# Sums of the weight quarters: from accumulating DMAs in DRAM to VectorE in the raw tiles

## The chip, the cores and the metric

One core of one Trainium2 chip runs the whole program in one launch. The metric is the device time in microseconds (us). Engines are called by these names: TensorE (PE: matmuls; PEld: its weight loads), VectorE (DVE), ScalarE (ACT), GpSimd (POOL) and SyncE (SP). SyncE and GpSimd issue the DMAs.

## The reference

A streaming-encoder block on 1024 tokens of width 1024, with 16 learned meta tokens ahead of them. The normalised stream is multiplied by `w_in`; its columns give, for four mLSTM heads (0 to 3) and four retention heads (4 to 7), queries, keys, values and an output gate. Each head runs a chunked scan over time and a norm, is gated, and `w_out` brings the heads back. A gated MLP with a causal convolution follows.

```python
    proj = up @ w_in
    (ml_q, ml_k, ml_v, ml_o, ml_i, ml_f, rt_q, rt_k, rt_v, rt_g) = jnp.split(proj, offs, axis=-1)
    ...
    h_ml = jax.nn.sigmoid(ml_o.astype(jnp.float32)) * h_ml
    ...
    h_rt = jax.nn.silu(rt_g.astype(jnp.float32)) * h_rt
    mixed = jnp.concatenate([h_ml, h_rt], axis=-1).astype(u.dtype)
    return (mixed @ w_out)[:, n_pad:]
```

Everything is float32.

## The kernel before, in words

**Products.** A float32 matrix is split into two float32r parts, `hi` (a cast on ScalarE) and `lo` (the rest, a subtraction on VectorE), and a product is three matmuls, hi x hi, hi x lo, lo x hi (`mm3s`). Most large products use the seven products of Strassen's scheme in Winograd's form: a weight is cut into four quarters, and seven products of quarters, or of sums of quarters, with blocks of the stream replace eight. The sums of the stream (S1 to S4) are made once; the sums of the weights, T1 = W11 + W12, T2 = T1 + W22, T3 = W12 + W22 and T4 = W21 + T2, are made for every head.

**Stages.** After a first norm (0 to about 82 us) the heads run from about 82 to 866 us in the order 4, then pairs (0, 1), (2, 3), (5, 6), then 7. For head 4 queries and keys come from plain products (`q4_group`). For the others `wino_fm("q", h)` makes queries and keys, `wino_fm("o", h)` the gate; `v_steps(p)` makes the values of a pair. Each of these is seven products in the order of `ROWS`. A head's products are merged with the scan tasks of the head before (`merge`, `group`), so that TensorE has both. From 866 us the output projection and the MLP follow; a planner with a model of the chip's times then orders each engine's queue from what the program emits, and each engine works through its own queue in that order.

**Weights on their way.** All loads stand in one list, `units`. `need(key, ahead)` issues units up to the one that is needed and two more. A unit takes a raw tile (`raw`, 128 x 1024 float32, 512 KB, two in a ring), loads it by SyncE's queue (L199), casts it into a tile `hi` (L201) and subtracts into a tile `lo` (L202). There are three pairs of tiles `hi`, `lo`, of 128 x 1024 each. A head of `wino_fm` has four units: W11 with W21, two units of sums, and W22 alone (half a tile). Between them stand, in the same ring, the `m` units (`last_two`: the last two tokens' part of `w_out`, scaled on ScalarE into a pair of split tiles and added to `accd` in DRAM by GpSimd, L243) and the `r` units (`first_right`: splits a block of the mixed heads and stores it).

**Weight sums.** `insum` makes the sums of one weight in DRAM by GpSimd's queue: a copy of the four quarters to `gs` (for values `vs`; L264), then four accumulating DMAs (`add`, L248). `job()` issues one weight's sums, at the start of the next group of heads. The same queue makes the sums of `w_out` and `w_down` (`wsum`; L255, L248).

**Meta tokens.** The values of the 16 meta tokens are made from the unsplit weights: `meta()` loads `w_vp[p]` again, in eight pieces of 256 KB through two halves of a slot (`vm`, L611), and multiplies by `ug` (L614).

**Scan.** `scan_b` copies the numerator out of the bank `num` on ScalarE (L1079) and the denominator's column `den` on VectorE (L1081).

Of the kernel before, what the change touches and what calls it, by code (L numbers as in the profile page):

```python
# [17 lines left out]
P = 128  # L18
# [7 lines left out]
DV = 256  # L26
# [39 lines left out]
def body(ctx, tc, h_in, vecs, cst, mask_in, rot, w_v0, w_vp, w_g, w_out, w_up, w_gate, w_down, out):  # L66
# [52 lines left out]
    vz = st.tile([P, 2, DV], F32, name="vz")  # L119
# [38 lines left out]
    nc.scalar.activation(warm[:, 0:1], epsc, AF.Square)  # L158
    for i in range(2):
        nc.sync.dma_start(w0raw[i], w_v0[i])  # L160
    nc.sync.dma_start(cs, cst)
# [16 lines left out]
    def unit(key, src, n=UN):  # L178
        units.append((key, src, n))
# [6 lines left out]

    def issue(upto):
        while issued[0] < min(upto, len(units)):
            u = units[issued[0]]
            issued[0] += 1  # L190
            if callable(u[1]):
                ready[u[0]] = u[1]()
                continue
            key, src, n = u
            nm = "_".join(str(k) for k in key)
            raw = raw_tile(nm)
            c = n // len(src)
            for i, x in enumerate(src):
                nc.sync.dma_start(raw[:, i * c:(i + 1) * c], x)  # L199
            hi, lo = split_tiles(nm)  # L200
            nc.scalar.copy(hi[:, :n], raw[:, :n])  # L201
            nc.vector.tensor_tensor(lo[:, :n], raw[:, :n], hi[:, :n].bitcast(F32), ALU.subtract)  # L202
            ready[key] = (hi, lo, raw)
# [12 lines left out]
    gsum = {i: dram.tile([P, 4 * HB], F32, name=f"gs{i}") for i in range(1, 17)}  # L216
# [3 lines left out]
    def u_fm(kind, h, extra=()):  # L220
        i = GI[kind, h]
        w, q = w_g[i], gsum[i]
        a = [[w[:, HB:3 * HB]], [q[:, :2 * HB]], [q[:, 2 * HB:]], [w[:, :HB]]]
        for j, x in enumerate(a):
            unit((kind, h, j), x, UN if j < 3 else HB)
            if j in (1, 2) and len(extra) > j - 1:
                units.append(extra[j - 1])

    def u_vp(p):
        w, q = w_vp[p], vsum[p]  # L230
        for j, (x, o) in enumerate(((w, 1), (w, 2), (q, 0), (q, 1), (q, 3), (w, 0), (q, 2))):
            unit(("vp", p, j), [x[:, o * UN:(o + 1) * UN]])

    def last_two(k):
        raw = raw_tile(f"m{k}")
        nc.sync.dma_start(raw, w_out[k])
        for t, x in enumerate(split_tiles(f"m{k}")):
            x = x.bitcast(F32)
            nc.scalar.activation(x, raw, AF.Copy, scale=mm[:, k, t:t + 1])
            if k == 8:  # L240
                nc.sync.dma_start(accd[t], x)
            else:
                G.dma_start(accd[t], x, accum_op=ALU.add)  # L243
# [17 lines left out]
    def insum(w, q, n, cuts):  # L261
        for i in range(cuts):
            c = 4 * n // cuts
            dep(G.dma_start(q[:, i * c:(i + 1) * c], w[:, i * c:(i + 1) * c]), last["pace"], True)  # L264
        b = lambda x, o: x[:, o * n:(o + 1) * n]
# [5 lines left out]
    jobs = []  # L271

    def job():
        if jobs:
            jobs.pop(0)()

    def j_fm(kind, h):
        i = GI[kind, h]
        jobs.append(lambda: insum(w_g[i], gsum[i], HB, 1))

    def j_vp(p):
        jobs.append(lambda: insum(w_vp[p], vsum[p], UN, 2))
# [6 lines left out]
    def first_right(k):  # L289
        a = raw_tile(f"fr{k}")  # L290
        hi, lo = split_tiles(f"fr{k}")
        nc.sync.dma_start(a, mxd[k])
        nc.scalar.copy(hi[:, :HB], a[:, :HB])
        nc.vector.tensor_tensor(lo[:, :HB], a[:, :HB], hi[:, :HB].bitcast(F32), ALU.subtract)
        nc.vector.tensor_tensor(a[:, HB:], a[:, :HB], a[:, HB:], ALU.subtract)
        nc.sync.dma_start(rone[k][:, :HB], hi[:, :HB].bitcast(F32))
        nc.sync.dma_start(rone[k][:, HB:], lo[:, :HB].bitcast(F32))
        nc.sync.dma_start(diff[k], a[:, HB:])
# [3 lines left out]
    def m_units(h):  # L302
        return [(("m", h, b), lambda k=2 * h + b: last_two(k), 0) for b in range(2)]

    def r_units(*ks):
        return [(("r", k), lambda k=k: first_right(k), 0) for k in ks]

    q4 = w_g[GI["q", 4]]
    unit(("q4", 0), [q4[:, HB:3 * HB]])
    unit(("q4", 1), [q4[:, 3 * HB:], q4[:, :HB]])  # L310
# [9 lines left out]
    u_fm("q", 7, r_units(2, 3))  # L320
    u_fm("v", 7, r_units(4, 5))
    u_fm("o", 7, m_units(6))
    units += r_units(6, 7)
# [59 lines left out]
    for u, s in fu:  # L383
        units.append((fseq[u] + (s,), lambda u=u, s=s: fstep(u, s)))
# [82 lines left out]
    def v4_group(c, tag):  # L467
# [3 lines left out]
        if c == 0:  # L471
# [4 lines left out]
            t = vz.rearrange("p a b -> p (a b)")[:META, :nv]  # L476
# [12 lines left out]
    def q4_group(i, half, j0, j1, tag):  # L489
        hi, lo, _ = need(("q4", i), 1 - i)  # L490
        pt = pp(f"pq4{i}{half}{j0}", tag)[:, :j1 - j0]
        for kb in range(KB):
            u = UB[f"{half + 1}{kb // 4 + 1}"]
            mm3(pt, tuple(x[:, kb * P:(kb + 1) * P] for x in (hi, lo)), tuple(x[:, kb % 4, j0:j1] for x in u), kb == 0, kb == KB - 1)
        nc.scalar.copy(raws[i][:, half * 512 + j0:half * 512 + j1], pt)

    ROWS = [("x", "11", 0, 0), ("y", "12", 0, 1), ("x", "S2", 1, 0), ("y", "S1", 1, 1), ("x", "S3", 2, 1), ("y", "S4", 3, 0), ("x", "22", 2, 0)]
# [13 lines left out]
    def wino_fm(kind, h, chunks, dst):  # L511
        get = gbanks(f"{kind}{h}")
        steps = []
        for n, (b, xb_, ui, hf) in enumerate(ROWS):
            for ci, (j0, j1) in enumerate(chunks):
                def step(n=n, b=b, xb_=xb_, ui=ui, hf=hf, ci=ci, j0=j0, j1=j1):
                    hi, lo, _ = need((kind, h, ui), 2)
                    u = UB[xb_]
                    pt = get(b, ci)[:, :j1 - j0]
                    mm3s(pt, [tuple(x[:, hf * HB + k * P:hf * HB + (k + 1) * P] for x in (hi, lo)) for k in range(4)],  # L520
# [41 lines left out]
    def v_steps(p):  # L562
# [14 lines left out]
        for n, (bk, xb_, _, _) in enumerate(ROWS):  # L577
            for cp in range(4):
                def step(n=n, bk=bk, xb_=xb_, cp=cp):
                    hi, lo, _ = need(("vp", p, n), 2)  # L580
# [6 lines left out]
                             [tuple(x[:, k * DV:(k + 1) * DV] for x in (hi, lo)) for k in range(4)], fresh and cp % 2 == 0, n in (1, 5, 6))  # L587
# [13 lines left out]
        def meta():  # L601
            x = vslot(ids[0, 1], f"vm{p}")
            q = 0
            for s in range(2):
                pv = pp(f"pvm{p}_{s}", "tr")
                for r in range(2):
                    o = WB[f"{r + 1}{s + 1}"] * UN
                    for kk in range(2):
                        y = x[:, q % 2 * 512:q % 2 * 512 + 512]
                        q += 1  # L610
                        nc.sync.dma_start(y, w_vp[p][:, o + kk * 512:o + kk * 512 + 512])  # L611
                        for i in range(2):
                            k = 2 * kk + i
                            nc.tensor.matmul(pv[32 * k:32 * k + 32, :DV], ug[:, 4 * r + k, :], y[:, i * DV:(i + 1) * DV],  # L614
                                             start=r == 0, stop=r == 1, tile_position=(0, 32 * k))
                quads(vz[:META, s], pv, DV)
        return steps, meta

    vcount = [0]
    VZ = {h: int(h in (1, 3, 6)) for h in HEADS}  # L620

    def v_split(h, c):
# [9 lines left out]
        elif c == 0:  # L632
            src = vz[:META, VZ[h]]
        else:
            src = vtile[h][c > 4][:, (c - 1) % 4 * DV:(c - 1) % 4 * DV + DV]
# [419 lines left out]
    def scan_b(h, c):  # L1055
# [15 lines left out]
        num.append(vz[:, VZ[h]] if c == 0 else vtile[h][c > 4][:, (c - 1) % 4 * DV:(c - 1) % 4 * DV + DV])  # L1071
# [8 lines left out]
        if h < H:  # L1080
            V.tensor_copy(den[:L, c:c + 1], pn[:L, DV:DV + 1])  # L1081
# [90 lines left out]
    need(("q4", 0), 0)  # L1172
# [16 lines left out]
    job()  # L1189
# [4 lines left out]
    job()  # L1194
# [58 lines left out]
    def group(steps, n, start=0, stop=None):  # L1253
        job()
        merge(steps, take(n), start, stop)

    group(o_steps(4), 5, 5)
    for p, (a, b) in enumerate(PAIRS):
        group(qk_steps(a), 7)
        steps, meta = v_steps(p)  # L1260
        group(steps[:12], 99, 0, 10)
        tables_load(a)
        meta()
# [3 lines left out]
        if p:  # L1267
            wsum("w", wjobs.pop(0))
        merge(steps[12:], take(5), 6)
        group(o_steps(a), 5)  # L1270
        if p:
            wsum("w", wjobs.pop(0))
        group(qk_steps(b), 99)
        if p:
            wsum("w", wjobs.pop(0))
# [3 lines left out]
        side += tasks(b)  # L1279
        group(o_steps(b), 5, 5)  # L1280
    wsum("w", wjobs.pop(0))
    group(qk_steps(7), 7)
    wsum("w", wjobs.pop(0))
# [618 lines left out]
```

## Time and profile before

| | |
|---|---|
| time, median of two runs | 1701.41 us (1700.43 to 1702.4) |
| profiled execution | 1706.06 us, span 1704.1 us |
| TensorE busy, share of the span | 91% |
| VectorE, ScalarE, GpSimd busy | 65%, 49%, 11% |
| mean granted TensorE clock | 0.946 |
| data moved by DMA | 303.02 MB, 178 GB/s |

The span is from the first to the last instruction of the profiled execution, and about 2 us lie around it. Busy time is a share of the whole span, which is made of stages with different limits. The granted clock is a share of TensorE's full speed. A wait row reads: engine, tile and line, what ended the wait, then us in total, how often, and the longest. A row of the groups reads: line, engine, operation, out <- in, shapes, count, then busy us and mean ns of one, then idle time before it and what ended it. A row of DMA issues: out <- in, queue, count, KB each, median us from issue to landing.

### The profile page before, as it was taken

The page shows a single profiled execution, that of the slowest core. Times are in us where ns is not written, and L with a number is a line of the kernel's source. Part 1 is how long each engine was busy: PE and PEld are TensorE (multiplying, and loading weights), DVE is VectorE, ACT ScalarE, POOL GpSimd, SP SyncE. Part 2 cuts the span into 40 slices and gives each one's busy share as a digit, 9 for nine tenths or more (in the row PEclk, how much of TensorE's full clock was granted, in tenths as well). Part 3 has the DMA queues.
Part 4 walks back from the last instruction along what each step waited for, and adds up shares of the span by engine and source line. Part 5 has one row for each costly group of instructions (what it writes and reads, how often), then busy time and mean ns, then how long its engine had stood idle before and what let it go on. Part 6 is the DMA issues. An engine that isn't in the chain of part 4 may idle for free.

```text
span 1704.1 us, 26448 instructions
## 1 busy us (share of the span) xinstructions
PE 1543.8 (91%) x9999; PEld 1398.7 (82%) x9999; DVE 1104.5 (65%) x2322; ACT 836.3 (49%) x1658; POOL 192.0 (11%) x270
## 2 busy tenths in 40 slices
PE   5989788799787978888789999999999999999998
PEld 5988778697777968787668889998899999888888
DVE  7675656475465735557478767876666666578757
ACT  5445547583566435454634544654434444444434
POOL 0201001112122112221000000022222000000000
PEclk8999899799989989889879999999999999999999
DMA  6756468878799887997993422588777222673312
GB/s 219 151 160 163 116 167 199 187 185 216 179 234 213 218 193 202 255 242 216 360 320 122 134 80 78 186 203 225 209 186 183 83 85 85 241 252 107 97 62 99
DMA packets 126079, 303.02 MB, mean 178 GB/s; under 512 B 13320, under 2 KB 36560, under 8 KB 124624
## 3 DMA queue, kind: packets, MB, share of 16 engines
q1 hardware_dynamic: 95152, 201.64, 35.8%
q0 software_dynamic: 30656, 99.63, 28.9%
q8 instruction: 78, 1.28, 0.3%
q14 instruction: 49, 0.40, 0.1%
q10 hardware_dynamic: 144, 0.07, 0.0%
HBM read 250.92 MB, written 136.36 MB: 227 GB/s over the span
## 4 chain that ended last, share of the span: by engine, by line
PE 63%; DMA 20%; issue 6%; DVE 6%; ACT 4%; POOL 1%; SPq 1%; DVEq 0%; POOLq 0%; ACTq 0%
DMA accd<-lo_m 2%; DMA A<-scr 2%; PE pdx L450 2%; PE pdx L451 2%; PE pdx L452 2%; PE pup_x L451 2%; PE pga_x L451 2%; PE pup_x L452 2%; PE pup_x L450 2%; PE pga_x L452 2%; PE pga_x L450 2%; DMA gs<-w_g_d 2%; PE pwx L451 2%; DMA diff<-raw_fr 2%; PE pwx L450 2%
## 5 line engine op out<-in xcount | busy, mean ns | idle before, releaser
L354 ACT CAST hi_up<-raw_up 128x512 fp32r<-128x512 f32 (+1 forms) x52 | 36.4, 719 | 106.9 <-PE pga_z L451 60.2
L202 DVE TENSOR_TENSOR lo_o<-raw_o,hi_o 128x1024 fp32r<-128x1024 f32 (+1 forms) x32 | 34.8, 1088 | 73.7 <-ACT hi_o L201 53.4
L450 PE MATMUL pup_x<-uh_g,hi_up 128*128 128x256 f32 (+1 forms) x240 | 67.1, 282 | 1.2 <-ACT uh_g L1302 1.2
L451 PE MATMUL pup_x<-ul_g,hi_up 128*128 128x256 f32 (+1 forms) x240 | 67.1, 281 | 0.1
L355 DVE TENSOR_TENSOR lo_ga<-fraw_ga,hi_ga 128x512 fp32r<-128x512 f32 (+1 forms) x52 | 42.0, 810 | 37.5 <-ACT hi_ga L354 37.3
L452 PE MATMUL pup_x<-uh_g,lo_up 128*128 128x256 f32 (+1 forms) x240 | 66.2, 282 | 0.0
L355 DVE TENSOR_TENSOR lo_up<-raw_up,hi_up 128x512 fp32r<-128x512 f32 (+1 forms) x52 | 41.3, 810 | 36.1 <-ACT hi_up L354 35.2
L201 ACT CAST hi_o<-raw_o 128x1024 fp32r<-128x1024 f32 (+1 forms) x32 | 30.0, 937 | 63.2 <-DMA raw_o<-w_g_d 17.1
L202 DVE TENSOR_TENSOR lo_q<-raw_q,hi_q 128x1024 fp32r<-128x1024 f32 (+1 forms) x30 | 32.8, 1095 | 41.5 <-ACT hi_q L201 22.9
L355 DVE TENSOR_TENSOR lo_d<-rd,hi_d 128x1024 fp32r<-128x1024 f32 (+1 forms) x34 | 37.7, 1114 | 32.9 <-ACT hi_d L354 32.8
L354 ACT CAST hi_ga<-fraw_ga 128x512 fp32r<-128x512 f32 (+1 forms) x52 | 36.4, 719 | 45.0 <-PE pup_z L451 22.9
L451 PE MATMUL pdx<-ul_d,hi_d 128*128 128x512 f32 (+1 forms) x156 | 58.1, 375 | 0.0
L452 PE MATMUL pdx<-uh_d,lo_d 128*128 128x512 f32 (+1 forms) x156 | 57.6, 373 | 0.0
L354 ACT CAST hi_d<-rd 128x1024 fp32r<-128x1024 f32 (+1 forms) x34 | 32.4, 960 | 48.5 <-PE pdy L451 32.6
L255 POOL DMA_DIRECT2D wsd<-w_down_d x33 | 20.0, 774 | 289.2 <-DVE s2up L1551 288.5
L451 PE MATMUL pdy<-ul_d,hi_d 128*128 128x512 f32 x132 | 51.9, 393 | 0.0
L452 PE MATMUL pdy<-uh_d,lo_d 128*128 128x512 f32 x132 | 51.3, 389 | 0.0
L201 ACT CAST hi_q<-raw_q 128x1024 fp32r<-128x1024 f32 (+1 forms) x30 | 28.4, 948 | 43.2 <-DMA raw_q<-w_g_d 15.5
L450 PE MATMUL pdx<-uh_d,hi_d 128*128 128x512 f32 (+1 forms) x156 | 48.8, 374 | 0.0
L450 PE MATMUL pdy<-uh_d,hi_d 128*128 128x512 f32 x132 | 48.3, 392 | 0.0
L451 PE MATMUL pga_x<-ul_g,hi_ga 128*128 128x512 f32 x120 | 47.6, 397 | 0.0
L452 PE MATMUL pga_x<-uh_g,lo_ga 128*128 128x512 f32 x120 | 47.3, 394 | 0.0
(1702 smaller groups left out, 6345.7 us busy)
## 6 DMA issues: line engine op xcount, KB each, us to landing
raw_up<-w_up_d SPq DMA_DIRECT2D x22, 512.0 KB, 4.5
fraw_ga<-w_gate_d SPq DMA_DIRECT2D x22, 512.0 KB, 4.8
acts<-cv SPq DMA_DIRECT2D x44, 256.0 KB, 3.0
wsd<-w_down_d POOLq DMA_DIRECT2D x44, 256.0 KB, 6.8
rd<-wsd SPq DMA_DIRECT2D x22, 512.0 KB, 3.5
gs<-w_g_d POOLq DMA_DIRECT2D x32, 256.0 KB, 7.2
gs<-gs POOLq DMA_DIRECT2D x32, 256.0 KB, 6.4
raw_o<-gs SPq DMA_DIRECT2D x16, 512.0 KB, 7.2
```

The lines of the kernel that those rows point to most:

```text
L201: nc.scalar.copy(hi[:, :n], raw[:, :n])
L202: nc.vector.tensor_tensor(lo[:, :n], raw[:, :n], hi[:, :n].bitcast(F32), ALU.subtract)
L255: dep(G.dma_start(x, y), last["pace"], True)
L354: nc.scalar.copy(hi[:, o:o + n], x)
L355: nc.vector.tensor_tensor(lo[:, o:o + n], x, hi[:, o:o + n].bitcast(F32), ALU.subtract)
L450: m.append(nc.tensor.matmul(pt, ah, xh_, start=first and k == 0, stop=False, skip_group_check=True))
L451: nc.tensor.matmul(pt, ah, xl_, start=False, stop=False, skip_group_check=True)
L452: m.append(nc.tensor.matmul(pt, al, xh_, start=False, stop=last and k == n - 1, skip_group_check=True))
```

## The change

The sums of the 16 weights of queries, keys, gates and of head 7's values leave DRAM. A head now loads its four quarters once into both raw tiles, `a` (W11, W21) and `b` (W12, W22), and keeps them there until its last part is split. VectorE adds in place: T1, then T2 in W11's half, T3 in W12's, T4 in W21's. The values' sums (`vs`) stay with GpSimd.

A split is now made half by half (128 x 512): `half_tiles` hands out the two halves of a pair of split tiles one after the other, so there are six half buffers. `need` without `ahead` issues units as far as they fit into five halves from the one needed. An `m` unit still takes a whole pair; the `m` and `r` units of a head now come behind it, not within it.

The meta products load whole quarters (512 KB) through the ring of raw tiles as units of no size, and write either half of `vz`, which is laid out flat; head 4's meta values move to its second half. `den` is copied on ScalarE. `cs` is loaded ahead of `w0raw`. The sums of the value weights are issued by `insum(0)` ahead of the first group and `insum(p + 1)` in pair p. The eight `wsum("w")` jobs are issued by three calls in each pair, from the first pair on.

```diff
+    def half_tiles(nm):
+        if open_half:
+            return [x[:, HB:] for x in open_half.pop()]
+        open_half.append(split_tiles(nm))
+        return [x[:, :HB] for x in open_half[0]]
+
+    def halves(nm, src):
+        r = []
+        for i in range(src.shape[1] // HB):
+            hi, lo = half_tiles(f"{nm}_{i}")
+            x = src[:, i * HB:(i + 1) * HB]
+            nc.scalar.copy(hi, x)
+            nc.vector.tensor_tensor(lo, x, hi.bitcast(F32), ALU.subtract)
+            r.append((hi, lo))
+        return r
...
-    def need(key, ahead):
+    def need(key, ahead=None):
         if not order:
             order.update({u[0]: i for i, u in enumerate(units)})
-        issue(order[key] + 1 + ahead)
+        i = order[key]
+        if ahead is None:
+            if not place:
+                o = 0
+                for k, n, _ in units:
+                    place[k] = o - (k[-1] == 3 and n == 0), o + n
+                    o += n
+            j = place[key][0]
+            while i + 1 < len(units) - len(fu) and place[units[i + 1][0]][1] <= j + 5:
+                i += 1
+            ahead = 0
+        issue(i + 1 + ahead)
         return ready[key]
...
-    def u_fm(kind, h, extra=()):
-        i = GI[kind, h]
-        w, q = w_g[i], gsum[i]
-        a = [[w[:, HB:3 * HB]], [q[:, :2 * HB]], [q[:, 2 * HB:]], [w[:, :HB]]]
-        for j, x in enumerate(a):
-            unit((kind, h, j), x, UN if j < 3 else HB)
-            if j in (1, 2) and len(extra) > j - 1:
-                units.append(extra[j - 1])
+    def u_fm(kind, h, *extra):
+        w = w_g[GI[kind, h]]
+        nm = f"{kind}{h}"
+        raw = {}
+
+        def form(n):
+            if n == 0:
+                raw["a"] = loaded((nm, "a"), [w[:, HB:3 * HB]])
+                raw["b"] = loaded((nm, "b"), [w[:, 3 * HB:], w[:, :HB]])
+            a0, a1, b0, b1 = (raw[x][:, i * HB:(i + 1) * HB] for x in "ab" for i in (0, 1))
+            if n == 2:
+                V.tensor_tensor(a0, a0, b0, ALU.add)
+                t2, t1 = (half_tiles(f"{nm}_{i}") for i in (2, 3))
+                for t, add in ((t1, False), (t2, True)):
+                    if add:
+                        V.tensor_tensor(a0, a0, b1, ALU.add)
+                    nc.scalar.copy(t[0], a0)
+                    V.tensor_tensor(t[1], a0, t[0].bitcast(F32), ALU.subtract)
+                ready[kind, h, 3] = t1
+                return t2
+            if n == 4:
+                V.tensor_tensor(b0, b0, b1, ALU.add)
+            if n == 6:
+                V.tensor_tensor(a1, a1, a0, ALU.add)
+            return halves(f"{nm}_{n}", {0: a0, 1: a1, 4: b0, 5: b1, 6: a1}[n])[0]
+        for n in (0, 1, 2, 4, 5, 6):
+            unit((kind, h, n), 2 if n == 2 else 1, lambda n=n: form(n))
+            if n == 2:
+                units.append(((kind, h, 3), 0, lambda: ready[kind, h, 3]))
+        units.extend(extra)
...
-    j_fm("o", 4)
-    for p, (a, b) in enumerate(PAIRS):
-        for f, x in ((j_fm, ("q", a)), (j_vp, (p,)), (j_fm, ("o", a)), (j_fm, ("q", b)), (j_fm, ("o", b))):
-            f(*x)
-    for x in "qvo":
-        j_fm(x, 7)
...
+    def meta_raw(p, s, r):
+        pv = metab.setdefault((p, s), None) or pp(f"pvm{p}_{s}", "tr")
+        metab[p, s] = pv
+        o = WB[f"{r + 1}{s + 1}"] * UN
+        y = loaded(("vm", p, s, r), [w_vp[p][:, o:o + UN]])
+        for k in range(4):
+            nc.tensor.matmul(pv[32 * k:32 * k + 32, :DV], ug[:, 4 * r + k, :], y[:, k * DV:(k + 1) * DV],
+                             start=r == 0, stop=r == 1, tile_position=(0, 32 * k))
+        if r:
+            quads(vz[:META, s * DV:(s + 1) * DV], pv, DV)
...
-    u_fm("o", 4)
+    u_fm("o", 4, *v_units(0, 0))
     prev = 4
     for p, (a, b) in enumerate(PAIRS):
         u_fm("q", a)
         u_vp(p)
-        u_fm("o", a, m_units(prev))
-        u_fm("q", b, r_units(0, 1) if p == 2 else ())
-        u_fm("o", b, m_units(a))
+        u_fm("o", a, *v_units(p, 1), *m_units(prev))
+        u_fm("q", b, *(r_units(0, 1) if p == 2 else ()))
+        u_fm("o", b, *(v_units(p + 1, 0) if p < 2 else ()), *m_units(a))
         prev = b
...
-            V.tensor_copy(den[:L, c:c + 1], pn[:L, DV:DV + 1])
+            nc.scalar.copy(den[:L, c:c + 1], pn[:L, DV:DV + 1])
...
     def group(steps, n, start=0, stop=None):
-        job()
         merge(steps, take(n), start, stop)
 
+    def wpace(n):
+        for _ in range(min(n, len(wjobs))):
+            wsum("w", wjobs.pop(0))
+
+    insum(0)
     group(o_steps(4), 5, 5)
```

More of the change, by code (lines that the diff above doesn't have):

```diff
@@ L176, in body, with unit @@
     issued = [0]
-    def unit(key, src, n=UN):
-        units.append((key, src, n))
+    def unit(key, size, make):
+        units.append((key, size, make))
     def raw_tile(nm):
@@ L190, in issue, with loaded, u_load, make @@
             issued[0] += 1
[L191 to L203, printed above, removed]
+            ready[u[0]] = u[2]()
     order = {}
-    def need(key, ahead):
+    place = {}
+    def need(key, ahead=None):
         if not order:
             order.update({u[0]: i for i, u in enumerate(units)})
-        issue(order[key] + 1 + ahead)
-        return ready[key]
+        i = order[key]
[10 more added lines that the diff above has]
+        issue(i + 1 + ahead)
+        return ready[key]
+    def loaded(key, srcs):
+        nm = "_".join(str(k) for k in key)
+        raw = raw_tile(nm)
+        o = 0
+        for x in srcs:
+            nc.sync.dma_start(raw[:, o:o + x.shape[1]], x)
+            o += x.shape[1]
+        return raw
+    def u_load(key, *srcs):
+        def make():
+            raw = loaded(key, srcs)
+            return halves("_".join(str(k) for k in key), raw)
+        unit(key, 2, make)
     GI = {("q", h): i for i, h in enumerate(HEADS)}
@@ L259, in wsum, with insum @@
         add(d73[:, :HB], d65[:, :HB])
[L261 to L265, printed above, removed]
+    def insum(p):
+        w, q = w_vp[p], vsum[p]
+        for i in range(2):
+            dep(G.dma_start(q[:, 2 * i * UN:2 * (i + 1) * UN], w[:, 2 * i * UN:2 * (i + 1) * UN]), last["pace"], True)
+        b = lambda x, o: x[:, o * UN:(o + 1) * UN]
         add(b(q, 1), b(w, 3))
@@ L269, in insum @@
         add(b(q, 2), b(q, 0))
[L271 to L282, printed above, removed]
     dcount = [0]
@@ L586, in step @@
                     m = mm3s(pt, [tuple(x[:, k, j0:j0 + P] for x in u) for k in range(4)],
[L587 removed]
+                             [tuple(x[:, k % 2 * DV:(k % 2 + 1) * DV] for x in w[k // 2]) for k in range(4)], fresh and cp % 2 == 0, n in (1, 5, 6))
                     if cp % 2 == 0:
@@ L599, in v_steps @@
                 steps.append(step)
[L601 to L617, printed above, removed]
+        return steps
     vcount = [0]
-    VZ = {h: int(h in (1, 3, 6)) for h in HEADS}
+    VZ = {h: int(h in (4, 1, 3, 6)) for h in HEADS}
     def v_split(h, c):
```

88 lines of the change are left out of this document (41 added, 47 removed).

## The prediction, made before the changed kernel was seen

> **What bounds the kernel now.** I read the page's busy shares and 40 slices first, then busy times by stage, the page's chain by engine, then the chain and the waits of the one stage that the change touches.
>
> ```profile
> PE 1543.8 (91%) x9999; PEld 1398.7 (82%) x9999; DVE 1104.5 (65%) x2322; ACT 836.3 (49%) x1658; POOL 192.0 (11%) x270
> PE   5989788799787978888789999999999999999998
> PEclk8999899799989989889879999999999999999999
> DMA  6756468878799887997993422588777222673312
> 82.00:866.00 784.00, 653.42 (x4780) 610.23 (x4778) 453.96 (x1233) 418.41 (x914) 124.70 (x166) 0.90 0.81 208
> 1081.00:1704.00 623.00, 613.83 (x3610) 542.68 (x3609) 433.80 (x696) 278.20 (x497) 55.43 (x79) 1.00 0.53 154
> PE 63%; DMA 20%; issue 6%; DVE 6%; ACT 4%; POOL 1%; SPq 1%; DVEq 0%; POOLq 0%; ACTq 0%
> ```
>
> A row of the table by stage gives length, busy time (and count) of TensorE, its weight loads, VectorE, ScalarE and GpSimd, then granted clock, DMA share, GB/s. From 1081 us on (the gated MLP) TensorE is busy 613.8 of 623 us at full clock; nothing there changes. From 82 to 866 us (the heads) it stands idle for 784 - 653 = 131 us, its clock is 0.90, VectorE is busy 58%, and the DMA engines 81%. All of the change but some lines at the start lies here. What sets the end in this stage:
>
> ```profile
> by line: issue 13.1%; DMA accd<-lo_m 5.3%; DMA A<-scr 5.2%; DMA gs<-w_g_d 4.1%; DMA diff<-raw_fr 3.9%; DMA raw_o<-w_g_d 3.5%; DMA raw_q<-w_g_d 3.0%; DMA raw_fr<-mxd 2.4%; DMA accd<-hi_m 2.4%; DMA raw_o<-gs 2.2%; DMA vm<-w_vp_d 2.0%; DMA raw
> ...
> 206.22 7.44 DMA gs<-w_g_d
> ...
> 239.25 11.22 DMA accd<-lo_m
> ...
> 250.55 1.24 DVE lo_q L202
> ```
>
> That is the chain, its shares of the 784 us and three pieces of it (start, length): a weight sum `gs` on GpSimd's queue, behind it the accumulating store `accd` of the last two rows, behind that the split of the next head's weights, for which TensorE waits. Transfers, not engines, come last. TensorE's idle time is spread over many such waits; these are the largest, with the GpSimd queue's own:
>
> ```profile
> PE pvm L614 <- DMA vm<-w_vp_d: 13.6, 5, 3.7
> PE n L440 <- DVE den L1081: 12.4, 5, 4.7
> PE po1y L450 <- ACT hi_o L201: 6.3, 1, 6.3
> POOL gs L248 <- DMA gs<-w_g_d: 150.4, 29, 12.9
> ```
>
> **Removed: the sums in DRAM.** Sixteen times the change drops a 1 MB copy to `gs` and four accumulating transfers of 256 KB, and each head's weights are then read once (1 MB) instead of 1.75 MB.
>
> ```profile
> q0 software_dynamic: 20515, 69.56, 44.0%
> q1 hardware_dynamic: 44129, 93.06, 36.5%
> gs<-w_g_d POOLq DMA_DIRECT2D x28, 256.0 KB, 7.4
> gs<-gs POOLq DMA_DIRECT2D x28, 256.0 KB, 6.8
> raw_q<-w_g_d SPq DMA_DIRECT2D x7, 512.0 KB, 6.8
> accd<-lo_m POOLq DMA_DIRECT2D x13, 512.0 KB, 9.4
> L264 POOL DMA_DIRECT2D gs<-w_g_d x14 | 8.0, 573 | 96.9 <-DVE v L598 44.3 <-DVE sig L529 35.6 <-DVE pt L1035 8.7
> raw_up<-w_up_d SPq DMA_DIRECT2D x22, 512.0 KB, 4.5
> ```
>
> In the stage: 14 copies of 1.05 MB and 56 adds of 0.26 MB are 29.4 of the 69.6 MB of GpSimd's queue, so 0.42 x 44% = 19% of the DMA engines' time. Of SyncE's 93 MB about 14 x 0.79 = 11 MB go, 4% more. The share of 0.81 becomes about 0.58 over the same length. Four terms follow.
>
> (1) `gs` on the chain: 4.1 + 2.2% of 784 us = 49 us. Something else is late soon after each, so the bounds are 0 and -49; I take half, -25. (2) Of the chain, `accd`, the tables `A`, `diff`, `raw_fr` and the weight loads are 25.7% = 201 us. A 512 KB load lands in 6.8 us here and in 4.5 us in the MLP, where the share is 0.53, that is 0.66 of the time. If all of it came through, -60 us; bounds 0 and -60, taken -30. (3) "issue" is 13.1% = 103 us, most of it seen on GpSimd's queue, which loses 70 of its 166 transfers (28 + 28 + 14). Scaled, that is -43 us; it overlaps (1), so bounds 0 and -43, taken -15. (4) Clock: a clock of 0.90 over 784 us is worth at most 78 us. With idle time down by a tenth or more the clock goes up a little; bounds 0 and -40, taken -8.
>
> **Where a page would price the clock otherwise.** Two stretches around the start of a head, and TensorE's three waits within the second:
>
> ```profile
> 195.00:206.00 11.00, 9.66 (x83) 9.45 (x81) 4.72 (x12) 2.62 (x5) 0.51 (x1) 1.00 0.44 152
> 206.00:224.00 18.00, 13.28 (x79) 10.59 (x80) 2.19 (x4) 5.12 (x8) 3.27 (x4) 0.82 0.87 234
> 206.50 0.63 PE L614 MATMUL pvm<-vm,ug 128*32 128x256 f32 x4 [1.84 <-DMA vm<-w_vp_d]
> 218.82 0.39 PE L450 MATMUL po0x<-uS3h,hi_o 128*128 128x258 f32 x1 [2.33 <-ACT hi_o L201]
> 221.46 1.07 PE L614 MATMUL pvm<-vm,ug 128*32 128x256 f32 x4 [1.90 <-DMA vm<-w_vp_d]
> ```
>
> Here waits of 1.8 to 2.3 us took the clock from 1.00 to 0.82. The Trainium skill (TensorE: Matmul & The Clock Gate, Part 1) says that the clock halves after an idle window of about 3.4 us; by that rule waits that shrink below it would cost no clock at all, and term (4) would be near its -40. The trace disagrees as far as it shows: shorter waits sufficed.
>
> **Moved: the meta products.** Per pair of heads `meta()` loads eight pieces of 256 KB into two halves of a slot, each waiting for the matmuls that read the piece before. Now four loads of 512 KB go through the ring of raw tiles, two halves of a head ahead. The five waits, 13.6 us, should mostly go; against that each load now holds one of the two raw tiles. Bounds -14 and +10; taken -8. The writer of `vz` moves with them, and head 4 uses the other half of it; that costs nothing, as only the addresses differ.
>
> **Added: vector work.**
>
> ```profile
> L295 DVE TENSOR_TENSOR raw_fr<-raw_fr 128x512 f32<-128x512 f32 x8 | 5.5, 690 | 7.5 <-DMA raw_fr<-mxd 7.5
> L202 DVE TENSOR_TENSOR lo_q<-raw_q,hi_q 128x1024 fp32r<-128x1024 f32 x21 | 25.6, 1219 | 34.6 <-ACT hi_q L201 16.0 <-DMA accd<-lo_m 15.8 <-ACT S_4h L1016 2.7
> L202 DVE TENSOR_TENSOR lo_o<-raw_o,hi_o 128x512 fp32r<-128x512 f32 x8 | 5.5, 690 | 26.9 <-DMA accd<-lo_m 16.2 <-ACT hi_o L201 10.7
> L201 ACT CAST hi_q<-raw_q 128x1024 fp32r<-128x1024 f32 x21 | 22.0, 1049 | 32.4 <-DMA accd<-hi_m 10.8 <-DMA raw_q<-w_g_d 4.8 <-DMA raw_q<-gs 4.8
> L293 ACT CAST hi_fr<-raw_fr x8: 601/620/648, 661.1 to 853.7; 128x512 fp32r<-128x512 f32 x8
> L1081 DVE COPY den<-n x36: 115/153/163, 230.2 to 575.2; 128x1 f32<-128x1 f32 x32, 16x1 f32<-16x1 f32 x4
> ```
>
> A head's parts are split today in three subtractions of 1.22 us and one of 0.69, 4.35 us; then in seven of 0.69 plus four adds of 0.69, 7.59 us: +3.24 us for each of 16 heads, 52 us. The 21 value units, in halves, add 21 x 0.16 = 3 us; 36 `den` copies of 0.15 us leave for ScalarE, -5.5. VectorE gets +50 us, from 58% to some 65-70% of the stage. ScalarE: 7 x 0.62 against 3 x 1.05 + 0.62 us, +0.57 for 16 heads, +4 for the value units, about +7 for `den`: +20 us. The cover is that both engines stand idle for over 40% of the stage; exposed in full it would be +50 (ScalarE's part runs beside it), covered in full 0. The page's chain has DVE at 6% of the span and its busy share is 65%, so a tenth of such work has been exposed; with the serial piece of the third product (add, cast, subtract, add, cast, subtract, about 4 us) that now hangs on one buffer I take +10. For `den` alone, TensorE's 12.4 us of waits may leave or grow with ScalarE's queue: bounds -12 and +12, taken 0.
>
> **Added: a wait on the raw pair.** Both raw tiles now stay taken from a head's first part to its last sum (the T4 sum in `a1`), so the next loads start only after the split of the seventh part. What stands between heads comes through the same two tiles: meta loads, then the two `m` units, then the next pair.
>
> ```profile
> sum 162.70, PE 134.65 PEld 121.99 DVE 75.22 ACT 86.85 POOL 24.35; mean PE 33.66 PEld 30.50 DVE 18.80 ACT 21.71 POOL 6.09
> sum 179.30, PE 144.74 PEld 139.49 DVE 113.06 ACT 112.92 POOL 35.12; mean PE 28.95 PEld 27.90 DVE 22.61 ACT 22.58 POOL 7.02
> ```
>
> These sum four output-gate heads (`po0`, `po1`, `po2`, `po5`: 40.7 us each, 5.8 a product) and five query-key heads (35.9 us, 5.1 a product). Six half buffers let the split of part seven run once the second product is done, five products or 25-29 us before the next head starts. From there a plain boundary needs one load and split, 6.8 + 0.62 + 0.69 = 8 us: hidden. A boundary with meta and `m` units needs three loads in a row, 3 x 6.8, two scalings (each about a cast of 1.05 us), and the split, about 24 us: just hidden now, and not if heads get as fast as 30 us (five sevenths is 21). ScalarE and VectorE run in order, so a split whose load is late also holds the evacuations and the scan's casts behind it, and TensorE waits for those. Bounds: 0, and 8 us at each of 16 boundaries, 128. Nearer to the first, by these lengths: +20.
>
> The earlier constants (`cs` ahead of `w0raw`), the second `q4` load and the spread of the `wsum` jobs (eight in both) I cost at nothing: they lie beside the first loads, and the same bytes move. The bound is 4 us either way.
>
> **Sum.** -25 - 30 - 15 - 8 - 8 + 10 + 20 = -56 us. The profiled execution took 1706.1 us (span 1704.1); the median of the two runs is 4.7 us less. So 1706 - 56 = 1650, as a median **1645 us**, 3.3% faster.
>
> **The rivals.** *The gain is eaten (no change).* The chain needs only new last links: the raw pair at +60 instead of +20, or the sums in DRAM were hidden anyway (VectorE and TensorE wait for `accd` and `A`, which stay), so that (1) to (3) give 25 instead of 70. Either gives 1685-1690. For it: `gs` itself is only 6% of the chain. Against: the queue it sits on is in most waits.
>
> *The raw pair decides (slower).* One mechanism: at every boundary the first cast of the next head waits in order on ScalarE for a load that could not start earlier; 16 x 6.8 = 109 us, plus half of VectorE's 50 us, since the casts and sums then come in a burst, less the 78 us of (1) to (4): +56, about 1757. It decides once the first load is issued less than about 8 us ahead of the first product. For it: the two tiles are all there is, and today's units free one after each split. Against: 25 us of lead by the lengths above.
>
> *The clock recovers too (faster still).* With waits shorter, term (4) comes near -40 and (2) near -45: 1645 - 32 - 15 = about 1598. Against: the rows quoted for the clock, where short waits halved it too. The Trainium skill (TensorE: Matmul & The Clock Gate, Part 1) would have the clock recover once waits are under its window.
>
> **How the numbers follow.** Forecast 0.55 (1612 to 1667 on its own), no change 0.20, slower 0.16, faster still 0.09. Two per cent of the time before, 34 us, is about what a measurement of this kernel can tell from no change; the forecast's band ends there. So faster 0.64, same 0.20, slower 0.16. The range reaches from 1600 to 1730: below it lies about half of the last case, above it most of the slower one.
>
> **What would show it.** Right: no `gs` transfers, GpSimd's queue near 40 MB in the heads' stage, DMA share there at or below 0.7; 512 KB loads landing in 5 to 6 us; the stage some 725 us long with TensorE idle for about 90 us and a clock above 0.91; 64 adds of about 0.69 us; no waits of `pvm` over 2 us. Wrong: TensorE or ScalarE waiting at head boundaries for the first raw load in long stretches (the raw pair), VectorE over 75% busy with TensorE waiting for it, or a DMA share as before.

## The result, and the profile after

The changed kernel takes 1635.6 us (1632.65 to 1638.61, two runs) against 1701.4 us: a ratio of 0.9613, 95% interval 0.9534 to 0.9692, 66 us or 3.9% faster. The prediction was 1645 us, 1600 to 1730. The page after, with its busy shares, slices and chain by engine:

```profile
PE 1516.6 (93%) x9999; PEld 1379.5 (84%) x9999; DVE 1145.1 (70%) x2421; ACT 845.8 (52%) x1764; POOL 131.2 (8%) x190
PE   5989898898798998988799999999999999999997
PEclk9989898999899999999799999999999999999999
DMA  5254677748765386649954223788775222953312
PE 71%; DMA 13%; DVE 7%; issue 5%; ACT 4%; SPq 0%; POOL 0%; DVEq 0%; ACTq 0%; POOLq 0%
```

The share of transfers in the chain fell from 20 to 13%, TensorE's rose from 63 to 71%. By stage (the heads from the first gate product to the first of the output projection; the MLP), with the transfers of the heads' stage below:

```profile
83.70:795.40 711.70, 624.22 (x4776) 591.07 (x4773) 491.93 (x1326) 428.33 (x1016) 72.27 (x96) 0.93 0.65 170
1011.50:1636.80 625.30, 615.76 (x3614) 544.63 (x3612) 434.66 (x698) 278.07 (x497) 55.43 (x79) 0.99 0.53 154
...
q1 hardware_dynamic: 39747, 80.06, 35.4%
q0 software_dynamic: 11970, 40.06, 29.3%
accd<-lo_m POOLq DMA_DIRECT2D x13, 512.0 KB, 8.9
raw_vp<-w_vp_d SPq DMA_DIRECT2D x9, 512.0 KB, 3.8
raw_q_a<-w_g_d SPq DMA_DIRECT2D x7, 512.0 KB, 6.9
```

The heads took 784 us and now take 712; the rest of the span is 5 us longer, 1.7 ahead of them and 3.3 behind. TensorE's idle time there went from 131 to 87 us, its clock from 0.90 to 0.93, the DMA share from 0.81 to 0.65, GpSimd's queue from 69.6 to 40.1 MB. VectorE has 38 us more. Not all transfers got quicker: the loads of the value units land in 3.8 instead of 6.1 us, but the stores `accd` in 8.9 instead of 9.4, and the first load of a query-key head in 6.9, where it was 6.8.

Four gate heads and five query-key heads (the same as in the prediction):

```profile
sum 120.10, PE 115.09 PEld 109.19 DVE 75.96 ACT 74.83 POOL 23.90; mean PE 28.77 PEld 27.30 DVE 18.99 ACT 18.71 POOL 5.97
sum 159.10, PE 127.81 PEld 121.78 DVE 101.58 ACT 110.99 POOL 16.88; mean PE 25.56 PEld 24.36 DVE 20.32 ACT 22.20 POOL 3.38
```

A gate head now takes 30.0 us (before: 40.7) with 1.3 us of it idle on TensorE. A query-key head takes 31.8 us (before: 35.9) and TensorE is still idle for 6.3 us of it. So of the 36 us of idle time in these nine heads 31 lie in the query-key heads, which come behind the meta loads and `m` units; the other 51 of the stage's 87 us lie elsewhere in it.

### The profile page after: what moved, and what is told of

It reads as the page before. It is cut to its first block, busy times and chain, and to the rows that moved or that the text cites. A ratio compares the mean times of both kernels' runs of the same rounds, so it can differ in the third digit from the quotient of the medians.

```text
span 1636.8 us, 26444 instructions
## 1 busy us (share of the span) xinstructions
PE 1516.6 (93%) x9999; PEld 1379.5 (84%) x9999; DVE 1145.1 (70%) x2421; ACT 845.8 (52%) x1764; POOL 131.2 (8%) x190
## 4 chain that ended last, share of the span: by engine, by line
PE 71%; DMA 13%; DVE 7%; issue 5%; ACT 4%; SPq 0%; POOL 0%; DVEq 0%; ACTq 0%; POOLq 0%
PE pdx L498 2%; PE pdx L499 2%; PE pdx L500 2%; PE pup_x L499 2%; PE pup_x L500 2%; PE pup_x L498 2%; PE pga_x L499 2%; PE pga_x L500 2%; PE pga_x L498 2%; PE pdy L499 2%; PE pdy L498 2%; PE pdy L500 2%; DMA accd<-lo_m 2%; DMA raw_vm<-w_vp_d 2%; PE pwx L499 2%
## 5 line engine op out<-in xcount | busy, mean ns | idle before, releaser
L498 PEld LDWEIGHTS pup_x<-uh_g,hi_up 128*128 128x128 f32 x240 | 45.8, 191 | 2.3 <-ACT uh_g L1332 1.4
L498 PE MATMUL pga_x<-uh_g,hi_ga 128*128 128x512 f32 x120 | 47.1, 393 | 0.0
L499 PEld LDWEIGHTS pup_x<-ul_g,hi_up 128*128 128x128 f32 x240 | 45.9, 191 | 1.1 <-DVE ul_g L1333 0.3
L500 PEld LDWEIGHTS pup_x<-uh_g,lo_up 128*128 128x128 f32 x240 | 45.0, 190 | 0.8
```

Source lines behind the costliest of these rows:

```text
L498: m.append(nc.tensor.matmul(pt, ah, xh_, start=first and k == 0, stop=False, skip_group_check=True))
L499: nc.tensor.matmul(pt, ah, xl_, start=False, stop=False, skip_group_check=True)
L500: m.append(nc.tensor.matmul(pt, al, xh_, start=False, stop=last and k == n - 1, skip_group_check=True))
```

## The experiments

A time is given as its ratio to the kernel before, run on the same chip; the time beside it is that ratio of 1701.4 us. The changed kernel itself is 0.9613 [0.9534, 0.9692]; its interval is the widest, as it rests on two runs. A difference to it is taken between the two ratios.

**The sums' transfers put back.** Two kernels: the changed one with the sums in DRAM made again for nobody, and the changed one that loads them from there.

```diff
+        dep(G.dma_start(q, w), last["pace"], True)
+        b = lambda x, o: x[:, o * HB:(o + 1) * HB]
+        add(b(q, 1), b(w, 3))
+        add(b(q, 3), b(w, 0))
+        add(b(q, 0), b(q, 1))
+        add(b(q, 2), b(q, 0))
...
     def group(steps, n, start=0, stop=None):
+        ghost()
```

> The changed kernel, with the 16 sums in DRAM issued again on GpSimd's queue at their old places (a 1 MB copy and four accumulating transfers each), and nobody reads them. Theory A (the gain is the traffic and the queue of these sums, terms 1 to 3 of the prediction): 50 to 80 us come back, 1685 to 1715 us, and 512 KB loads land in 6 to 7 us again. Rival B (the gain is the order of the units, the half buffers and the meta loads; the sums were hidden): within 15 us of the changed kernel, 1636 to 1650 us.

> The changed kernel with one part undone: the sums of the 16 weights are made in DRAM again and loaded from there; half buffers, order of the units, meta products through the ring, den on ScalarE stay as changed. Theory A: the traffic costs +50 to +80, the missing 64 adds and the raw pair that is no longer held give back 20 to 30: 1660 to 1700 us. Rival B: faster than the changed kernel or the same, 1600 to 1640 us.

`ghost_sums`: 0.9782 [0.9744, 0.9820], 1664 us, 29 us more than the changed kernel. `dram_sums`: 0.9820 [0.9769, 0.9871], 1671 us, 35 us more, although it has none of the 64 adds. Both speak against rival B; `ghost_sums` came out below theory A's 50 us.

**The sums taken out of the kernel before.** The reverse test, with nothing else changed:

```diff
-        a = [[w[:, HB:3 * HB]], [q[:, :2 * HB]], [q[:, 2 * HB:]], [w[:, :HB]]]
+        a = [[w[:, HB:3 * HB]], [w[:, :2 * HB]], [w[:, 2 * HB:]], [w[:, :HB]]]
...
-        jobs.append(lambda: insum(w_g[i], gsum[i], HB, 1))
+        jobs.append(lambda: None)
```

> The kernel before without its 16 sums in DRAM: the units of sums load quarters of the weights as they are, so the weight sums are left out of the computation; nothing else changes, and nothing is added on VectorE. In the prediction's terms 1, 3 and the part of 2 and 4 that comes from the sums: -50 to -80 us, 1625 to 1655 us. If the gain needs the other parts (order, meta loads) as halves_only suggests: -20 to -40 us, 1665 to 1685 us.

0.9636 [0.9587, 0.9684], 1639 us: 62 us less, within theory A's figure. Its heads and GpSimd's DMA queue:

```profile
83.50:802.00 718.50, 632.21 (x4776) 589.68 (x4773) 455.58 (x1234) 414.67 (x912) 71.58 (x95) 0.94 0.68 184
...
q0 software_dynamic: 11924, 39.88, 28.5%
```

The old order, the old tiles and the old meta products are all there, and the stage is 718 us long with a clock of 0.94. So taking out the transfers of the sums alone is worth about as much as the whole change.

**Bytes or the queue?** The accumulating transfers wait for one another on GpSimd's queue, and other stores stand behind them. This kernel moves the same bytes, and the transfers of these 16 weights no longer wait for one another (the edit is against `ghost_sums`):

```diff
-        add(b(q, 1), b(w, 3))
-        add(b(q, 3), b(w, 0))
-        add(b(q, 0), b(q, 1))
-        add(b(q, 2), b(q, 0))
+        for j in range(4):
+            dep(G.dma_start(b(gsum2[i], j), b(w, j)), last["pace"], True)
```

> As ghost_sums, but the four accumulating transfers of each weight are plain copies of 256 KB to places of their own, so no transfer waits for another on GpSimd's queue, and the bytes are the same. If the bytes cost the time: as ghost_sums, 1660 to 1672 us. If it is the queue in which the accumulating stores stand behind waits: near the changed kernel, 1636 to 1648 us.

0.9907 [0.9876, 0.9938], 1686 us: 50 us more than the changed kernel, and 21 us more than with the chained transfers. So the cost does not need the waits in the queue: without them the time is longer. Whether they cost something by themselves is hidden behind what came in their place. GpSimd's queue (packets, MB, share of the DMA engines' time) and its groups of DMA issues in `ghost_sums`, then in `ghost_free`:

```profile
q0 software_dynamic: 20471, 69.38, 45.7%
...
gs<-w_g_d POOLq DMA_DIRECT2D x28, 256.0 KB, 6.9
gs<-gs POOLq DMA_DIRECT2D x28, 256.0 KB, 6.0
```

```profile
q0 software_dynamic: 16923, 69.52, 39.4%
...
gt<-w_g_d POOLq DMA_DIRECT2D x56, 256.0 KB, 10.2
```

And rows of the waits (engine and tile, what it waits for: sum, count, longest in us) of the changed kernel, of `ghost_sums` and of `ghost_free`:

```profile
PE tr L1157 <- DVE mx L1164: 10.5, 4, 6.1
DVE A L704 <- DMA A<-scr: 13.9, 4, 7.1
DVE A L705 <- DMA A<-scr: 11.4, 3, 6.4
```

```profile
PE tr L1177 <- DVE mx L1184: 28.8, 6, 9.9
DVE A L724 <- DMA A<-scr: 18.7, 4, 7.7
DVE A L725 <- DMA A<-scr: 18.4, 4, 9.4
```

```profile
PE tr L1176 <- DVE mx L1183: 30.9, 5, 16.2
DVE A L724 <- DMA A<-scr: 27.5, 3, 13.7
DVE A L723 <- DMA A<-scr: 8.1, 3, 3.8
```

With the sums' transfers back, VectorE stands 37 and 36 us for the scan's tables `A`, instead of 25, and TensorE's transposes wait 29 and 31 us, instead of 11, for what stands behind that on VectorE. So a part of the cost is the collision with loads that an in-order engine waits for. In the kernel before it shows as well: VectorE stands 34 us for the tables there and 14 us in `before_no_sums`. The further 21 us of `ghost_free` are not in these rows, which are as long as those of `ghost_sums`. Its transfers of one weight are sent together and land in 10.2 us instead of 6 to 7; but they are also plain copies where the others accumulate, with fewer packets for the same bytes, and the two were not separated.

**The vector work.**

```diff
-                V.tensor_tensor(a0, a0, b0, ALU.add)
...
-                    if add:
-                        V.tensor_tensor(a0, a0, b1, ALU.add)
...
-            if n == 4:
-                V.tensor_tensor(b0, b0, b1, ALU.add)
-            if n == 6:
-                V.tensor_tensor(a1, a1, a0, ALU.add)
```

> The changed kernel without its 64 adds on VectorE: the parts are split from the quarters as they are, so the weight sums are left out of the computation. The prediction's term for the vector work: exposed at a tenth to a fifth of 44 us, so 5 to 12 us faster, 1624 to 1631 us. Rival C (VectorE is the new bound of the heads): 25 to 50 us faster, 1585 to 1610 us. Rival D (fully covered): within 3 us.

0.9519 [0.9485, 0.9554], 1620 us, 16 us less, with the two intervals just overlapping; above the prediction's 5 to 12, far from rival C. It prices more than the adds: without the sums the split of the third product no longer needs the head's second load, for which VectorE waits 12 us in all in the changed kernel. In the changed kernel these adds took what the rows of before had said, 680 to 689 ns; one of their eight groups for queries, keys and gates, with VectorE's wait for the second load:

```profile
L263 DVE TENSOR_TENSOR raw_q_a<-raw_q_a,raw_q_b 128x512 f32<-128x512 f32 x7 | 4.8, 689 | 9.9 <-DMA raw_q_b<-w_g_d 6.1 <-issue 3.9
```

Then half of the adds on GpSimd (`G.tensor_tensor` in the last two places of the diff above):

> The changed kernel with the adds for T3 and T4 (32 of 64) on GpSimd instead of VectorE. Without any of the 64 adds it was 16 us faster. If what they cost is VectorE's time, half of it comes back: 4 to 8 us faster, 1628 to 1632 us. If it is the length of the row of sums ahead of the splits, GpSimd's queue, which waits for transfers, makes it 5 to 30 us slower.

0.9711 [0.9684, 0.9738], 1652 us, 17 us more, with the two intervals just touching. One add took about twice as long, and it stood in a queue that waits for other things:

```profile
L273 POOL TENSOR_TENSOR raw_q_b<-raw_q_b 128x512 f32<-128x512 f32 x7 | 12.5, 1781 | 58.2 <-DVE raw_q_a L263 30.5 <-DVE mv L1099 11.7 <-DMA raw_q_b<-w_g_d 10.1
```

**The raw pair.** The two raw tiles are held by a head, then lent to the meta loads and both `m` units. The timeline of the changed kernel at the start of the query-key head of head 3, which begins at 424.4 us (start, length, engine): the last scaling of the first `m` unit, the head's first load, its first split, the last scaling of the second `m` unit, the second load, and the first sum:

```profile
413.58 1.14 ACT L293 ACTIVATE lo_m<-raw_m,mm 128x1024 f32<-128x1024 f32 x1
414.74 0.33 SPq L236 DMA_DIRECT2D raw_q_a<-w_g_d  x1
421.69 0.62 ACT L200 CAST hi_o<-raw_q_a 128x512 fp32r<-128x512 f32 x1 [0.73 <-DMA raw_q_a<-w_g_d]
423.56 1.16 ACT L293 ACTIVATE lo_m<-raw_m,mm 128x1024 f32<-128x1024 f32 x1
425.49 4.34 SPq L236 DMA_DIRECT2D raw_q_b<-w_g_d  x2
442.46 0.69 DVE L263 TENSOR_TENSOR raw_q_a<-raw_q_a,raw_q_b 128x512 f32<-128x512 f32 x1
```

The first load is issued as soon as the first `m` unit is scaled, and its split starts at 421.7, 2.7 us ahead of the product. The second load is issued only at 425.5, behind the last scaling of the second `m` unit and after the product has begun, and the first sum follows at 442.5. Two ways to loosen the row:

```diff
-        u_fm("o", a, *v_units(p, 1), *m_units(prev))
+        u_fm("o", a, *v_units(p, 1))
...
-        u_fm("o", b, *(v_units(p + 1, 0) if p < 2 else ()), *m_units(a))
+        u_fm("o", b, *(v_units(p + 1, 0) if p < 2 else m_units(a)))
```

Here all `m` units go between the last value units of the next pair (and those of head 5 stay). In the second kernel one stays behind each gate head and the other goes there (both of head 5 stay again).

> The changed kernel with the m units of heads 4, 0, 1, 2, 3 moved from behind the gate heads to between the value units of the next pair. If the row meta load, m load, first load through the two raw tiles holds the query-key heads (the raw pair term), their first products come earlier: 10 to 20 us faster, 1616 to 1626 us. If those heads wait for the scan and the banks instead: within 5 us; if the value units lose more by sharing three pairs of split tiles with m units: 5 to 15 us slower.

> The changed kernel with the m units spread: one behind each gate head, the others (one for pair 0, two for the later pairs) between the last value units. m_in_values took 15 us off, with query-key heads of about 29 us but value heads 12 us longer in all. If the chain meta load, m load, first load is the cost, one m unit per boundary gives most of that and the value units lose less: 1610 to 1622 us. If one m unit behind a head costs as much as two: 1622 to 1636 us.

`m_in_values`: 0.9523 [0.9486, 0.9560], 1620 us. `m_split`: 0.9447 [0.9419, 0.9474], 1607 us (its own runs: median 1613.8 us), 28 us less than the changed kernel and the fastest of all. The rows of `m_split`: the heads' stage, then its query-key heads and its gate heads, the same nine as above; and the three stretches of the value products, in the changed kernel and in `m_split`.

```profile
84.90:767.50 682.60, 614.92 (x4777) 582.28 (x4774) 492.09 (x1329) 420.83 (x1012) 72.14 (x96) 0.95 0.67 179
...
sum 150.00, PE 135.33 PEld 130.94 DVE 112.94 ACT 112.77 POOL 13.70; mean PE 27.07 PEld 26.19 DVE 22.59 ACT 22.55 POOL 2.74
sum 123.00, PE 114.42 PEld 107.01 DVE 88.69 ACT 77.01 POOL 23.62; mean PE 28.61 PEld 26.75 DVE 22.17 ACT 19.25 POOL 5.91
```

```profile
sum 180.90, PE 171.67 PEld 164.70 DVE 142.84 ACT 110.48 POOL 16.08; mean PE 57.22 PEld 54.90 DVE 47.61 ACT 36.83 POOL 5.36
sum 166.00, PE 158.70 PEld 152.55 DVE 116.63 ACT 101.26 POOL 21.52; mean PE 52.90 PEld 50.85 DVE 38.88 ACT 33.75 POOL 7.17
```

TensorE's idle time in the five query-key heads fell from 31.3 to 14.7 us, with the same bytes. In length these heads lost only 9 us and the gate heads gained 3; the value stretches lost 15. A head's products are merged with the scan of another, so work moves between the stretches, and the gain can't be put down to one of them.

That the order of the `m` units costs 28 us is shown. That it does so through the two raw tiles is not. At head 3 of the changed kernel these are the longest waits of TensorE, then VectorE's for transfers:

```profile
PE tr L1157 <- DVE mx L1164: 6.1, 1, 6.1
PE n L488 <- ACT den L1113: 5.8, 1, 5.8
```

```profile
DVE A L704 <- DMA A<-scr: 7.1, 1, 7.1
DVE A L705 <- DMA A<-scr: 6.4, 1, 6.4
DVE raw_q_b L273 <- DMA raw_q_b<-w_g_d: 0.7, 1, 0.7
```

VectorE stands 13.5 us for the scan's tables and 0.7 us for the late second load, and `mx` comes behind both on VectorE, `den` behind ScalarE's part of the tables. In `m_split` VectorE waits 5.1 us for the tables at head 3. Moving an `m` unit also takes its load and its stores away from the tables' loads, so a collision at the boundary is a rival to the raw pair, and no run separates the two.

**The smaller parts, each undone by itself.** The meta products through the slot again; `den` on VectorE; the sums of `w_out` at their old places.

> The changed kernel with one part undone: the meta products load eight pieces of 256 KB through the slot again, at their old place behind the first value products, and not through the ring. The prediction's term for the move was -8 us (bounds -14 and +10): 5 to 14 us slower than the changed kernel, 1641 to 1650 us. If the meta loads only take the raw tiles from the heads' own loads: 5 to 10 us faster.

> The changed kernel with the den column copied on VectorE again. The prediction took 0 with bounds -12 and +12. If TensorE's waits for den were VectorE's queue: 5 to 12 us slower, 1641 to 1648 us; if they were the scan's own chain: within 4 us of 1636 us.

> The changed kernel with the eight sums of w_out issued at their old places (three in each of pairs 2 and 3, two around head 7) and not from the first pair on. The prediction costed the spread at nothing, 4 us either way: 1632 to 1640 us. If the load late in the stage matters (DMA share 0.94 there before): 5 to 15 us slower, 1641 to 1650 us.

`meta_back`: 0.9664 [0.9628, 0.9699], 9 us slower. TensorE's waits for `pvm`, which were 13.6 us before and are 7.6 us in the changed kernel, are no longer than that with the old meta products either, in `before_no_sums` and then in `meta_back`:

```profile
PE pvm L613 <- DMA vm<-w_vp_d: 6.9, 3, 3.8
```

```profile
PE pvm L646 <- DMA vm<-w_vp_d: 6.1, 3, 3.1
```

So these waits fell as the sums' transfers went, not by the move. `den_back`: 0.9608 [0.9567, 0.9649], the same. `pace_back`: 0.9656 [0.9611, 0.9700], 7 us slower. `meta_back` and `pace_back` overlap with the changed kernel's wide interval, so neither cost is shown, only that it is small.

**All of these undone together,** leaving the half buffers and the units behind the heads:

> The changed kernel with four parts undone together: sums in DRAM, meta products through the slot, den on VectorE, old places of the sums of w_out. Left are the half buffers and the m and r units behind the heads. The parts undone alone cost 35, 9, 0 and 7 us; if they add, 1636 + 51 = 1687 us, and the rest of the gain (14 us) belongs to the half buffers and the order. If they overlap: 1670 to 1680 us. If they need each other: at or above the time before, 1701 us.

1.0097 [1.0069, 1.0124], 1718 us: slower than before. The parts do not add: undone one by one they cost 35, 9, 0 and 7 us, 51 in sum, and undone at once 82. Beside the old traffic, the half buffers and the new order of the units together lose 1%. ScalarE waits longer for loads of weights here; the first row, of query-key heads, is 13.9 us in `dram_sums` and 4.8 in the kernel before:

```profile
ACT hi_q L200 <- DMA raw_q<-gs: 27.4, 7, 8.1
ACT hi_o L200 <- DMA raw_o<-gs: 19.4, 6, 8.8
```

## Why the prediction was right, and where its terms were off

**The transfers, terms (1) to (4).** Forecast -78 us together. Taken out of the kernel before they gave -62; put back into the changed kernel, +29 chained and +50 at once. The direction holds, and so does the main step: it is these transfers that hold the stage. Term (2) was sized by a rule that did not hold evenly: all loads were to land in 0.66 to 1 of their time, but `accd` and the first load of a query-key head hardly got quicker (9.4 to 8.9, 6.8 to 6.9 us); why was not tested. (Its bound was also miscounted: 0.34 of 201 us is 68, not 60.) Of the counts, GpSimd's 40 MB, a share below 0.7, 87 us of idle time and a clock of 0.93 came as said. The queue as a cause, which term (3) and the chain of 206 to 252 us suggested, found no support: without waits between the transfers and with the same bytes the time was longer. How much of the 62 us is rate and how much is collision with the tables and stores was not separated.

**The rival on the clock.** A clock near full, and with it 1598 us, did not come: the clock is 0.93 with TensorE's waits for `pvm` at most 2.8 us long.

```profile
PE pvm L353 <- DMA raw_vm<-w_vp_d: 7.6, 4, 2.8
PE n L488 <- ACT den L1113: 6.5, 4, 5.8
```

The Trainium skill (TensorE: Matmul & The Clock Gate, Part 1) puts the limit at an idle window of about 3.4 us. This run does not decide that rule, as waits over the limit are left here too (the second row's longest is 5.8 us). Stretches of 3.4 us from the kernel before, around the rows that the prediction shows, say more:

```profile
203.90:207.30 3.40, 1.56 (x13) 0.97 (x12) 0.00 (x0) 0.00 (x0) 1.08 (x2) 0.99 0.67 210
207.30:210.70 3.40, 3.40 (x17) 3.40 (x17) 0.00 (x0) 2.19 (x2) 0.58 (x1) 0.51 0.87 189
...
217.50:220.90 3.40, 0.74 (x4) 0.54 (x4) 1.23 (x1) 1.04 (x1) 0.00 (x0) 1.00 0.81 210
220.90:224.30 3.40, 2.84 (x12) 2.03 (x13) 1.26 (x3) 0.36 (x1) 0.81 (x1) 0.50 0.63 124
```

After 3.4 us in which TensorE was busy for 1.56 us, and again after 3.4 us with 0.74 us, the next 3.4 us ran at half the clock, and no single wait there was longer than 2.33 us. In these two places a stretch that was idle in part was enough.

**The vector work.** +10 forecast, 16 measured by `no_adds`, at the edge of the noise and with the wait for the second load in it. If the term was too small, the likely step is that it took the whole span's exposed share, a tenth, for work that stands in a serial row ahead of the splits; `pool_adds`, which lengthens that row, fits this but moves the adds behind GpSimd's waits as well.

**The meta products.** -8 forecast, 9 by `meta_back`, within the noise. The way was wrong: the waits for `pvm` were to go by the move, but they fall to 6 or 7 us with the old meta products too once the sums are gone, and 7.6 us of them are left, so "no waits of `pvm` over 2 us" was wrong. That 8 and 9 agree is luck until a run shows what the move changes.

**`den` and the spread of the sums.** `den` at 0 was right. The spread was costed at nothing with 4 us either way and came out at 7, within the noise.

**The raw pair.** +20 forecast, "just hidden" at a boundary with meta and `m` units. `m_split` has 28 us back by taking one `m` unit from that boundary, so the place fits, and the size is not far off: the query-key heads behind such boundaries are idle for 6.3 us each, the gate heads, whose boundary is plain, for 1.3. The mechanism is open, as the waits at head 3 show. The slower rival was to decide once the first load is issued less than about 8 us ahead of the first product. At the five query-key heads it was issued 8.3 to 9.7 us ahead (at head 3 at 414.7 against 424.4 us), far less than the 25 us of the prediction's lengths for a plain boundary but just enough, as its "just hidden" said. TensorE waited for a head's first split at heads 2, 5 and 7 alone, for 2.2, 3.2 and 3.7 us. So the rival's condition was not met, and its long waits did not come. At head 3 it is the second load that comes late, which neither the term nor the rival named.

**What was not a term.** Half buffers and the new order of `m` and `r` units were not priced by themselves. `halves_only` has them cost 16 us beside the old traffic, and `m_split` shows that the order has a price with the traffic gone too. The pieces do not add up: -62 from the transfers, +16 for the adds, -9 and -7 for meta and spread come to -62, near the measured -66, but with the 28 us that `m_split` gives back counted as a cost they come to -34. Each was measured in another kernel, and what joins them stays open. So -56 against -66 is partly luck: the transfers' -78 was too much, and the +30 set against it was right in sign with neither part shown in size.

**A reading that was off.** The prediction called its rows TensorE's largest waits in the heads' stage. Two longer ones than its third, `pq3y` (7.5 us) and `pq1x` (6.4 us), both waiting for VectorE to empty a bank, are missing there; no term rests on them.

## What to carry to other kernels

Here a stage's transfers took 81% of the DMA engines and engines that feed TensorE waited for them in order. Moving the sums of weights out of DRAM was then worth more (62 us) than the vector work that it added (16 us); in such a stage it is worth trying. A term for the saved bytes is better tested by leaving them out of the old kernel than by a rule on landing times. Where buffers are held longer, look at what else goes through the same ring at the next boundary and try to spread it: that order was worth 28 us here, whatever the mechanism. And a wait that a change was meant to remove should be looked up in a run without that change, as `pvm` shows.

## What the runs showed of the hardware that was not expected

The same bytes cost more in one form than in another: transfers of 256 KB in DRAM landed in 10.2 us as plain copies sent together, four beside a copy of 1 MB, and in 6.0 to 6.9 us as accumulating ones, one behind the other. The kernel was 21 us slower with the bunch, at a lower mean DMA share (0.73 against 0.79).

```profile
83.60:830.10 746.50, 635.50 (x4777) 601.20 (x4774) 491.74 (x1324) 425.47 (x1013) 124.61 (x165) 0.91 0.79 201
```

```profile
84.30:846.00 761.70, 635.19 (x4776) 598.37 (x4774) 497.49 (x1331) 423.86 (x1012) 108.53 (x166) 0.91 0.73 200
```

The first row is the heads' stage of `ghost_sums`, the second that of `ghost_free`. So between these two kernels the mean share of the DMA engines does not tell which transfers cost more. An add of 128x512 took 1.29 to 1.78 us on GpSimd, where VectorE took 0.69.
